# Attention by pairs of heads, with scores transposed, in a hybrid transformer layer

## The chip, the cores and the metric

The kernel runs on one core of a Trainium2 chip. The metric is the device time of one execution in microseconds (us): the median of the runs, each the time of that core. The core has five engines that run side by side, each with its own queue of instructions that it works off in order: TensorE (PE, matrix products, results in PSUM; PEld is its weight load), VectorE (DVE), ScalarE (ACT), GpSimd (POOL) and SyncE (SP), which here issues the transfers (DMAs) between the chip's memory and the core's SBUF.

## The reference

One layer over a prompt of 1024 tokens and a sample of 64 tokens that continues a cache of 256. A projection makes the columns of a recurrent mixer (RWKV, 8 heads of 64) and of a forgetting attention (FoX, 8 heads of 64); their outputs, side by side, go through one output projection, a gated residual, and a gated feed-forward part. The attention, which the change touches:

```python
s = einsum('bqhd,bshd->bhqs', q, k) * HEAD_DIM ** -0.5
decay_bias = lc_q[..., :, None] - lc_k[..., None, :]   # cumulated log-forget values
p = softmax(where(pos_k <= pos_q, s + decay_bias, -inf), axis=-1)
y_fox = einsum('bhqs,bshd->bqhd', p, v)
...
mix = concatenate([y_rwkv, y_fox], axis=-1) @ w_out
x = x + gt1 * mix
ffn = (silu(h2 @ w_ffn_gate) * (h2 @ w_ffn_up)) @ w_ffn_down
```

Everything is float32. The prompt attends to itself; the sample attends to the cache and to itself.

## The kernel before

The tokens are worked on in two halves: half 0 has prompt tokens 0 to 511, half 1 prompt tokens 512 to 1023 and the 64 of the sample (576 columns). The stages follow one another: conditioning and the projections of half 0 and half 1 (`pmm`, to 668.6 us of the profiled execution), attention of half 0, attention of half 1 with the output projection of half 0 among it (`po`, whose last matmul starts at 894.2), output projection of half 1, feed-forward (`pfa` to `pfe`), and `down`.

A projection multiplies in fp32r (a faster float format) with each operand split in a high and a low part: three matmuls a step, high by high, low by high, high by low (`mm3`, L322 to L324). Within the projections a written list, `ORDER`, sets in which order the parts of the recurrent mixer (A, B, D, N) and of q, k, v (Q, q, K, k, V) of each pair of heads are handed to the scheduler, which then interleaves their instructions on each engine. B3 is the chain of the last pair of the recurrent mixer (its matmuls are `pS` and `pY`), N3 its normalisation (`y`, `pbs`, `plora`), with which half 1's part of `yscr` is written. q and k go to memory as `qx` and `kx`, split in high and low (rows 0 to 63 and 64 to 127) with four rows for the forget bias; v goes to `vscr`, split too (`put_v`).

Attention goes head by head (`attend`, eight heads a half, units of 256 queries). For 128 queries: scores `psc` with queries on the partitions (two fp32r matmuls for each 512 or 256 keys, L957 and L959, and a mask, L963); the row's maximum by a DVE reduction (`nm`); exponential with the row sum on ACT (`p`); division by the sum (DVE or ACT); then 128x128 blocks of `p` are turned by fp32 transposes (`ppt`, L987), so that keys lie on the partitions, split in high (`pth`, ACT) and low (`ptl`, DVE), and multiplied with the split values (`pav`, L1009, two matmuls for each block of 128 keys; the weights hold 64 high and 64 low columns of v, so the two halves of the result are added at the end, `fy`). `Pipe(2)` lets three units overlap. Half 0's `fy` goes to `yscr` in memory (L1021), from where `load_mix` reads it back into `mixt`, two buffers in turn, and splits it into `mixrh`, `mixrl`, `mixfh`, `mixfl` for the output projection.

In half 1 every head has operands in two sets, which the transfers of the next head fill. After the units of each head stands one output tile of half 0's output projection (`outproj`: 8 tiles, 24 matmuls `po` each). `residual_x` reads the layer's input for the residual.

The SP queue issues all these transfers in order: a transfer that waits holds up those behind it.

## Time and profile before

| | |
|---|---|
| median of 3 runs | 1691.39 us (1688.1 to 1692.68) |
| the profiled execution | 1687.64 us; span of the instructions 1685.9 us |
| granted TensorE clock, mean | 0.991 |
| busy: PE / DVE / ACT / POOL | 1621.7 / 1107.1 / 731.5 / 130.4 us |
| bytes moved, mean rate | 207.05 MB, 123 GB/s |
| last projection matmul starts | 668.2 us |
| transfer of half 0's last `fy` issued | 734.4 us |
| last matmul of half 0's output projection starts | 894.2 us |

A row of the profile names the source line, engine, operation, result and operands, then the shape. Matmuls overlap, so that the duration of one is longer than its cost in a row of many: that cost is the distance from one start to the next.

### The profile page before, as it was taken

The page shows a single profiled execution, that of the slowest core. Times are in us where ns is not written, and L with a number is a line of the kernel's source. Part 1 is how long each engine was busy: PE and PEld are TensorE (multiplying, and loading weights), DVE is VectorE, ACT ScalarE, POOL GpSimd, SP SyncE. Part 2 cuts the span into 40 slices and gives each one's busy share as a digit, 9 for nine tenths or more (in the row PEclk, how much of TensorE's full clock was granted, in tenths as well). Part 3 has the DMA queues.
Part 4 walks back from the last instruction along what each step waited for, and adds up shares of the span by engine and source line. Part 5 has one row for each costly group of instructions (what it writes and reads, how often), then busy time and mean ns, then how long its engine had stood idle before and what let it go on. Part 6 is the DMA issues. An engine that isn't in the chain of part 4 may idle for free.

```text
span 1685.9 us, 32908 instructions
## 1 busy us (share of the span) xinstructions
PE 1621.7 (96%) x12959; PEld 1420.0 (84%) x12959; DVE 1107.1 (66%) x2397; ACT 731.5 (43%) x1496; POOL 130.4 (8%) x308
## 2 busy tenths in 40 slices
PE   5999999999999999879999999999999999999999
PEld 3666666688888888647889899999999999999998
DVE  6577676768876754868877975555555556545545
ACT  4543564653545445757766633233333333211210
POOL 0102101030211002002110000000000000000000
PEclk9999999999999999979999999999999999999999
DMA  7535366541233344576554532222222225423313
GB/s 309 161 101 156 108 180 206 173 124 44 60 86 96 94 117 116 178 212 167 153 162 164 187 104 77 78 77 78 77 78 78 77 65 188 140 84 97 97 41 122
DMA packets 133576, 207.05 MB, mean 123 GB/s; under 512 B 62126, under 2 KB 70350, under 8 KB 133422
## 3 DMA queue, kind: packets, MB, share of 16 engines
q1 hardware_dynamic: 133422, 204.95, 39.9%
q8 instruction: 102, 1.67, 0.4%
q14 instruction: 52, 0.43, 0.1%
HBM read 157.65 MB, written 47.25 MB: 122 GB/s over the span
## 4 chain that ended last, share of the span: by engine, by line
PE 58%; ACT 3%; DVE 2%; issue 1%; DMA 1%; SPq 0%; POOL 0%; DVEq 0%; ACTq 0%
PE pd L1322 15%; PE pfe L1207 8%; PE pfc L1207 8%; PE pfa L1207 8%; PE pfb L1207 4%; PE pav L1009 2%; PE ppt L987 2%; PE po L322 2%; PE po L323 2%; PE po L324 2%; PE psc L957 1%; PE psc L959 1%; ACT p L969 1%; PE pmm L322 1%; PE pmm L323 1%
## 5 line engine op out<-in xcount | busy, mean ns | idle before, releaser
L322 PE MATMUL pmm<-hhi,whi 128*128 128x288 f32 (+1 forms) x624 | 220.0, 353 | 6.0 <-ACT pb L345 4.6
L323 PE MATMUL pmm<-hlo,whi 128*128 128x288 f32 (+1 forms) x624 | 215.7, 346 | 1.8 <-DVE hlo L300 1.8
L324 PE MATMUL pmm<-hhi,wlo 128*128 128x288 f32 (+1 forms) x624 | 213.0, 342 | 0.2 <-DVE wlo L244 0.2
L240 ACT CAST whi<-wraw 128x1024 fp32r<-128x1024 f32 (+2 forms) x116 | 99.1, 855 | 205.8 <-PE pd L1322 164.0
L1322 PE MATMUL pd<-al,whi 128*128 128x512 f32 (+1 forms) x528 | 172.4, 327 | 0.0
L1322 PE MATMUL pd<-ah,whi 128*128 128x512 f32 (+1 forms) x528 | 172.2, 326 | 0.0
L1322 PE MATMUL pd<-ah,wlo 128*128 128x512 f32 (+1 forms) x528 | 172.2, 326 | 0.0
L1326 DVE SCALAR_TENSOR_TENSOR x1t<-pd,mod,x1t 128x512 f32<-128x512 f32 x192 | 91.1, 498 | 106.5 <-PE pd L1322 105.8
L322 PEld LDWEIGHTS pmm<-hhi,whi 128*128 128x128 f32 x624 | 118.5, 190 | 22.6 <-ACT pb L345 7.6
L323 PEld LDWEIGHTS pmm<-hlo,whi 128*128 128x128 f32 x624 | 118.5, 190 | 13.9 <-DVE hlo L300 2.8
L324 PEld LDWEIGHTS pmm<-hhi,wlo 128*128 128x128 f32 x624 | 118.3, 190 | 11.2 <-issue 1.7
L244 DVE TENSOR_TENSOR wlo<-wraw,whi 128x1024 fp32r<-128x1024 f32 (+2 forms) x108 | 104.0, 963 | 28.3 <-ACT whi L240 26.1
L1322 PEld LDWEIGHTS pd<-ah,whi 128*128 128x128 f32 x528 | 99.0, 188 | 7.1
L1322 PEld LDWEIGHTS pd<-ah,wlo 128*128 128x128 f32 x528 | 99.0, 188 | 7.1
L1322 PEld LDWEIGHTS pd<-al,whi 128*128 128x128 f32 x528 | 99.1, 188 | 7.0
L1207 PE MATMUL pfc<-hh,hS 128*128 128x256 f32 (+1 forms) x352 | 101.8, 289 | 1.1 <-ACT hh L1109 1.1
L1207 PE MATMUL pfa<-hh,whi 128*128 128x256 f32 (+1 forms) x352 | 102.0, 290 | 0.0
L1207 PE MATMUL pfc<-hh,lS 128*128 128x256 f32 (+1 forms) x352 | 101.8, 289 | 0.0
L1207 PE MATMUL pfa<-hl,whi 128*128 128x256 f32 (+1 forms) x352 | 101.7, 289 | 0.0
L1207 PE MATMUL pfa<-hh,wlo 128*128 128x256 f32 (+1 forms) x352 | 101.5, 289 | 0.0
L1207 PE MATMUL pfc<-hl,hS 128*128 128x256 f32 (+1 forms) x352 | 100.7, 286 | 0.0
L1154 ACT CAST hS<-wraw 128x512 fp32r<-128x512 f32 x88 | 53.6, 620 | 62.7 <-PE pfc L1207 61.5
(370 smaller groups left out, 4260.2 us busy)
## 6 DMA issues: line engine op xcount, KB each, us to landing
wraw<-in_w_in_dram SPq DMA_DIRECT2D x52, 512.0 KB
wada<-in_w_ada_dram SPq DMA_DIRECT2D x48, 512.0 KB
as<-actscr SPq DMA_DIRECT2D x22, 544.0 KB
wraw<-in_w_gate_dram SPq DMA_DIRECT2D x22, 512.0 KB
wraw<-in_w_up_dram SPq DMA_DIRECT2D x22, 512.0 KB
wraw<-in_w_down_dram SPq DMA_DIRECT2D x40, 256.0 KB
wraw<-in_w_out_dram SPq DMA_DIRECT2D x16, 512.0 KB
actscr<-sg SPq DMA_DIRECT2D x22, 288.0 KB
```

The costliest lines, as they stand in the source:

```text
L240: nc.scalar.copy(hi, src)
L244: eng.tensor_tensor(lo, src, hi.bitcast(F32), op=ALU.subtract)
L322: nc.tensor.matmul(ps[0:M, 0:n], whi[:, k, 0:M], xhi[:, k, off:off + n], start=(k == 0), stop=False)
L323: nc.tensor.matmul(ps[0:M, 0:n], whi[:, k, 0:M], xlo[:, k, off:off + n], start=False, stop=False)
L324: nc.tensor.matmul(ps[0:M, 0:n], wlo[:, k, 0:M], xhi[:, k, off:off + n], start=False, stop=(k == kt - 1))
L957: nc.tensor.matmul(pq[:, c:c + w], qs[:, q0 - t0:q0 - t0 + P], k1[:, k0 + c:k0 + c + w], start=True, stop=False, skip_group_check=True)
L987: nc.tensor.transpose(pt[0:rows, b - b0, t * P:t * P + qn], p[0:qn, pc:pc + rows], self.ident[0:qn, 0:qn])
L1009: nc.tensor.matmul(pv[:, 0:nq], w, pTs[b // 2][t][0:rows, b % 2, 0:nq], start=(b == 0 and t == 0), stop=(b == kb - 1 and t == 1))
L1154: nc.scalar.copy(w[x][0], src)
L1207: nc.tensor.matmul(ps, l[:, k], r[:, s, k], start=(first and k == 0 and y == 0), stop=(k == 3 and y == 2), skip_group_check=True)
L1322: nc.tensor.matmul(ps[:, 0:n], w[:, i], x[:, t:t + n], start=(i == 0 and y == 0), stop=(i == len(fs) - 1 and y == 2))
L1326: nc.vector.scalar_tensor_tensor(dst, ps[:, so - off:so - off + l], self.mod[:, 40 + o, b:b + 1], dst, op0=ALU.mult, op1=ALU.add)
```

## The change

Attention is worked off by pairs of heads. Scores are made twice. Once with the queries on the partitions in one fp32r matmul of 73 rows (`pmx`, high parts, the bias and a mask) only for the rows' maxima: DVE reduces each (`nmx`), one transpose (`pnm`) and two DVE operations put minus the maxima as further rows into the operand `qb`. Then transposed, keys on the partitions (`pst`, two fp32r matmuls and on the diagonal a mask), so that the exponential on ACT gives the weights as the value product needs them. The 312 transposes, the split of `p`, the split of v (`put_v`) and the division of each row go. The value product is plain fp32 on 64 columns a head, the two heads of a pair on column halves of the array (`pav`, 64x512); the weights are summed over the key blocks by adds one block behind (`acc`: in half 1 the second head's on POOL, else on DVE), a matmul with ones makes the sum over keys (`psm`), and one over it comes from ACT as exp(-ln). In half 1 `pss`, `pvs` are the sample's.

Half 0's pairs 0 to 2 stand in `ORDER` among half 1's last projections: `m` is the loads and maxima of a pair, `a` the rest. Pair 3 follows after them; half 1's pair 0 is loaded then, and its maxima stand beside pair 3. In half 1 (`att_second`) the order on PE is pinned as written: the maxima of the next pair and steps of three `po` matmuls stand among the blocks of the current pair, by the table `MIX`. There the operands `ka`, `qa`, `qb` of a head are single; `kb` and `qc` (for the maxima) are loaded one pair ahead. In the recurrent mixer the PSUM tag `ch` has one buffer instead of two; its place goes to `pv`.

```diff
         "Z0 T3 L D0 A0 ...
-... N1 V0 V1 B2 V2 Q2 N2 q2 K3 Q3 q3 P B3 K2 k3 k2 V3")
+... N1 V0 V1 B2 V2 Q2 N2 q2 m0 B3 K3 a0 Q3 q3 m1 K2 k3 a1 k2 V3 m2 N3 a2")
...
-            pm = [self.ps([P, 4, 2, 64], tag="ch", name="pM") for _ in range(2)]
+            pm = [self.ps([P, 4, 2, 64], tag=t, name="pM") for t in ("ch", "rb")]
...
-        self.put_v(j, vt, t0 // P, 4, P)
+        nc.sync.dma_start(self.vscr[j][:, t0 // P:t0 // P + 4], vt)
         if hf.smp:
-            self.put_v(j, vs.unsqueeze(1), 10, 1, SS)
+            nc.sync.dma_start(self.vscr[j][0:SS, 8], vs)
...
+    def att_get(self, j, hf):
...
+            g["tags"] = {"st": "st", "mx": "mx", "pv": "pv", "sm": "mx"}
...
+        k = self.rpool.tile([P, 4, 512], F32R, tag="At", name="ak")
+        g["ka"], g["kb"] = [k[:, h] for h in range(2)], [k[0:73, 2 + h] for h in range(2)]
+        t = self.rpool.tile([P, 4, 512], F32R, tag="kr", name="aq")
+        g["qa"], g["qb"] = [t[:, h] for h in range(2)], [t[0:73, 2 + h] for h in range(2)]
+        t = self.rpool.tile([P, 2, 512], F32R, tag="sv", name="qc")
+        g["qc"] = [t[0:73, h] for h in range(2)]
...
+        g["tags"] = {"st": "ra", "mx": "ra", "pv": "pv", "sm": "ra"}
+    def att_load(self, j, hf, g, part):
...
+            if part == 0:
+                ld(qc[0:64, 0:n], self.qx[hd, 64:128, q])
+                ld(qc[69:73, 0:n], self.qx[hd, 128:132, q])
+                ld(kb[0:64, 0:NK], self.kx[hd, 0:64, 0:NK])
+                ld(kb[69:73, 0:NK], self.kx[hd, 128:132, 0:NK])
+            elif part == 1:
+                ld(qb[0:64, 0:n], self.qx[hd, 0:64, q])
+                ld(qb[69:73, 0:n], self.qx[hd, 128:132, q])
+                for r in (0, 64):
+                    ld(qa[r:r + 64, 0:n], self.qx[hd, 64:128, q])
+                ld(ka[:, 0:NK], self.kx[hd, 0:128, 0:NK])
...
+    def att_max(self, j, hf, g):
+        nc, te = self.nc, self.te
+        nmx = self.nmx[j % 2]
+        kb, qc = g["kb"], g["qc"]
+        for h in range(2):
+            pc = self.tpool.tile([P, 4, 2], F32, tag="pc", name="pc") if hf.smp else None
+            for t in range(5 if hf.smp else 4):
+                smp = t == 4
+                qn, nk, k0 = (SS, 320, SP) if smp else (P, hf.t0 + (t + 1) * P, 0)
+                for x, c in enumerate(range(0, nk, 512)):
+                    m = min(512, nk - c)
+                    w = max(256, m)
+                    ps = self.ps([P, 512], tag=g["tags"]["mx"], name="pmx")
+                    te.matmul(ps[:, 0:w], qc[h][:, t * P:t * P + P], kb[h][:, k0 + c:k0 + c + w], start=True,
+                              stop=False, skip_group_check=True)
+                    if c + m == nk:
+                        d = 0 if smp else m - qn
+                        te.matmul(ps[0:qn, d:d + qn], self.identb[0:qn, 0:qn], self.cmask[0][0:qn, 0:qn], start=False,
+                                  stop=True, skip_group_check=True)
+                    dst = pc[:, t, x:x + 1] if hf.smp and not smp else nmx[0:qn, 32 * h + t:32 * h + t + 1]
+                    nc.vector.tensor_reduce(dst, ps[0:qn, 0:m], axis=AX.X, op=ALU.max, negate=True)
+                    yield
...
+    def att_rows(self, j, hf, g):
...
+        te.transpose(pt, self.nmx[j % 2], self.ident)
+        for h in range(2):
+            r = slice(32 * h, 32 * h + 5)
+            nc.vector.tensor_tensor(g["qb"][h][64:69, 0:nt * P].rearrange("p (t q) -> p t q", q=P),
+                                    pt[r].unsqueeze(1).to_broadcast([5, nt, P]),
+                                    self.ident[r, 32 * h:32 * h + nt].unsqueeze(2).to_broadcast([5, nt, P]), op=ALU.mult)
+    def att_main(self, j, hf, g):
...
+        blocks = [(b, max(0, b * P - t0)) for b in range(t0 // P + 4)]
+        acc = [g["acc"]() for _ in two]
+        pv = self.ps([P, 512], tag=tags["pv"], name="pav")
...
+        def scores(b, c0):
+            r = []
+            for h in two:
+                ps = self.ps([P, 512], tag=tags["st"], name="pst")
+                w = min(256, c0)
+                kc = slice(b * P, b * P + P)
+                diag = b * P >= t0
+                te.matmul(ps[:, w:512], ka[h][:, kc], qa[h][:, w:512], start=True, stop=False, skip_group_check=True)
+                te.matmul(ps[:, w:512], kb[h][:, kc], qb[h][:, w:512], start=False, stop=not diag, skip_group_check=True)
+                if diag:
+                    te.matmul(ps[:, c0:c0 + P], self.identb, self.cmask[1], start=False, stop=True, skip_group_check=True)
+                p = g["pt"]()
+                r.append((p, nc.scalar.activation(p[:, c0:512], ps[:, c0:512], AF.Exp)))
+                if h == 0:
+                    yield
+            done.append((b, c0, r))
+        def total(b, c0, r):
+            for h in two:
+                p, a = r[h][0], acc[h]
+                eng = nc.gpsimd if h and hf.smp else nc.vector
+                if b == 0:
+                    first.append(p)
+                elif b == 1:
+                    if c0:
+                        nc.gpsimd.tensor_copy(a[:, 0:c0], first[h][:, 0:c0])
+                    eng.tensor_tensor(a[:, c0:512], first[h][:, c0:512], p[:, c0:512], op=ALU.add)
+                else:
+                    eng.tensor_tensor(a[:, c0:512], a[:, c0:512], p[:, c0:512], op=ALU.add)
...
+        def values(group):
...
+                    mms.append(lambda b=b, c0=c0, h=h, p=p: te.matmul(
+                        pv[hs[h], c0:512], v[:, b, hs[h]], p[:, c0:512], start=(b == 0), stop=(b == blocks[-1][0]),
+                        skip_group_check=True))
...
+        done = []
+        for b, c0 in blocks:
+            for _ in scores(b, c0):
+                yield "h"
+            if len(done) > 1:
+                total(*done[-2])
+            yield "b"
+            if len(done) == 3:
+                values(done[:2])
+                del done[:2]
+            yield b
+        total(*done[-1])
+        values(done)
...
+        yield "v"
+        pd = self.ps([P, 512], tag=tags["sm"], name="psm")
+        for h in two:
+            te.matmul(pd[hs[h]], self.ones[:, 0:64], acc[h][:, 0:512], start=True, stop=True, skip_group_check=True)
+        fy = g["fy"]()
+        for c, m, a, d in ((0, 512, pv, pd),) + (((512, SS, pvs[:, 0], pvs[:, 1]),) if hf.smp else ()):
+            r = g["r"]()[:, 0:m]
+            nc.scalar.activation(r, d, AF.Ln)
+            nc.scalar.activation(r, r, AF.Exp, scale=-1.0)
+            nc.vector.tensor_tensor(fy[:, c:c + m], a, r, op=ALU.mult)
...
+    def proj_steps(self, hf):
...
+            for k in range(KT):
+                for y, (l, r) in enumerate(((wh, mh), (wh, ml), (wl, mh))):
+                    self.te.matmul(ps[:, 0:hf.n], l[:, k], r[:, k, 0:hf.n], start=(k == 0 and y == 0),
+                                   stop=(k == KT - 1 and y == 2))
+                if k == KT - 1:
+                    self.add_gated(ps, o, 16, hf, 0, hf.n)
+                yield
+    MIX = (1, 1, 1, 1, 1, 1, 1, 2)
+    def att_second(self, hf, h0):
+        fill = lambda it, n: [next(it, None) for _ in range(n)]
+        g = self.att_g
+        po = self.proj_steps(h0)
+        self.te.on = True
+        for j in range(4):
+            nxt, mx = None, iter(())
+            if j < 3:
+                nxt = self.att_get(j + 1, hf)
+                self.att_load(j + 1, hf, nxt, 0)
+                mx = self.att_max(j + 1, hf, nxt)
+            for b in self.att_main(j, hf, g):
+                if b == "v":
+                    if nxt:
+                        self.att_load(j + 1, hf, nxt, 2)
+                    fill(po, 4)
+                elif b in ("h", "b"):
+                    fill(mx, 1)
                 else:
+                    fill(po, self.MIX[b])
+                    fill(mx, b == 7)
+                if b == 7 and nxt:
+                    fill(mx, 99)
+                    self.att_load(j + 1, hf, nxt, 1)
+                    self.att_rows(j + 1, hf, nxt)
+                    fill(po, 2)
+            if j == 2:
+                self.load_mix(hf)
+            g = nxt
+        fill(po, 99)
+        self.te.on = False
...
+            self.att_ops(R(att, "attp", 1), 1)
+            self.tpool = MultiPool({t: R(att, "t" + t, b) for t, b in (("pc", 2),)})
+            self.att_pair(3, halves[0], "m")
+            self.att_g = g = self.att_get(0, halves[1])
+            for x in range(2):
+                self.att_load(0, halves[1], g, x)
+            main = self.att_main(3, halves[0], self.att0.pop(3))
+            mx = self.att_max(0, halves[1], g | {"tags": {"mx": "ra"}})
+            for b in main:
+                if b in range(4):
+                    for _ in range(5):
+                        next(mx, None)
             for b, f in late.values():
                 f(b())
+            self.att_rows(0, halves[1], g | {"tags": {"sm": "ra"}})
...
-            pb = {t: PB(att, "p" + t, b) for t, b in (("s1", 1), ("tr", 2), ("mm", 1), ("av", 1), ("s0", 1))}
+            self.pspool = MultiPool({t: PB(att, "p" + t, b) for t, b in (("st", 3), ("pv", 1), ("mm", 2), ("mx", 2))})
+            self.att_ops(R(att, "attp2", 1), 0)
+            self.att_load(0, halves[1], g, 2)
+            self.residual_x(halves[0])
+            self.load_mix(halves[0])
+            self.att_second(halves[1], halves[0])
```

Three places in the instructions' order. First PE about the last projection matmul. Before (`psc` is half 0's first head):

```order
2519 L322 MATMUL pmm<-hhi,whi 128x288
2520 L323 MATMUL pmm<-hlo,whi 128x288
2521 L661 MATMUL pS<-sv,kr 128x128
2522 L668 MATMUL pY<-kr,sv 128x128
2523 L324 MATMUL pmm<-hhi,wlo 128x288
2524 L861 MATMUL pkv<-ident,fv 128x128 x2
2525 L957 MATMUL psc<-k1x_7653,qsx_7651 128x256
2526 L959 MATMUL psc<-k2x_7654,q2x_7652 128x256
2527 L963 LDWEIGHTS identb
2528 L963 MATMUL psc<-cmask,identb 128x128
2529 L661 MATMUL pS<-sv,kr 128x128
2530 L668 MATMUL pY<-kr,sv 128x128
```

And now (`ak` and `qc` belong to half 0's pair 2; its maxima begin behind the last `pmm`, those of pairs 0 and 1 and their value products stand ahead of it):

```order
2660 L336 MATMUL pmm<-hhi,whi 128x288
2661 L337 MATMUL pmm<-hlo,whi 128x288
2662 L338 MATMUL pmm<-hhi,wlo 128x288
2663 L864 MATMUL pkv<-ident,fv 128x128 x2
2664 L1812 MATMUL pmx<-ak,qc 128x256
2665 L1812 LDWEIGHTS identb
2666 L1812 MATMUL pmx<-cmask_676,identb 128x128
2667 L1812 MATMUL pmx<-ak,qc 128x256
2668 L1812 LDWEIGHTS identb
2669 L1812 MATMUL pmx<-cmask_676,identb 128x128
2670 L417 MATMUL pbs<-y,bmean 128x288
2671 L1812 MATMUL pmx<-ak,qc 128x384
```

Where half 0's first head stood there is now its third pair.

Second, SP behind half 0's attention, from the transfers just before or at its last `yscr`. Before (`k1x`, `k2x`, `qsx`, `q2x`, `vsx` are half 1's first head's operands):

```order
412 L1043 DMA x_0_9112<-in_x_dram 128x1024 x3
413 L1031 DMA mixt<-yscr_71 128x512 x2
414 L915 DMA qsx_9133<-qx 128x576
415 L917 DMA k1x_9135<-kx 64x1344
416 L1021 DMA yscr_71<-fy 128x512
417 L917 DMA k1x_9135<-kx 64x1344
418 L920 DMA q2x_9134<-qx 64x576
419 L921 DMA k2x_9136<-kx 64x1344
420 L920 DMA q2x_9134<-qx 4x576
421 L921 DMA k2x_9136<-kx 4x1344
422 L923 DMA vsx_9137<-vscr_103 128x1280
423 L924 DMA vsx_9137<-vscr_103 64x128
```

And now (the operands of half 1's pair 0 have been issued ahead of these rows but for its values `vx`; `qcx_8489` and `kbx_8820` belong to pair 1):

```order
419 L1115 DMA yscr_71<-r_8723 128x512
420 L1200 DMA x_0_8772<-in_x_dram 128x1024
421 L1188 DMA mixt<-yscr_71 128x512
422 L958 DMA vx_8824<-vscr_103 128x1024
423 L959 DMA vx_8824<-in_cache_v_dram 128x256
424 L960 DMA vx_8824<-vscr_103 64x128
425 L1188 DMA mixt<-yscr_71 128x512 x2
426 L940 DMA qcx_8489<-qx 64x576
427 L940 DMA qcx_8489<-qx 4x576
428 L940 DMA kbx_8820<-kx 64x1344
429 L1188 DMA mixt<-yscr_71 128x512 x2
430 L940 DMA kbx_8820<-kx 4x1344
```

The read-back of half 0's output and its residual now stand ahead of the next pair's operands, where before a head's operands stood between them.

Third, PE at the start of half 1's attention. Before (behind the last `pav` of half 0):

```order
2794 L1009 MATMUL pav<-ptl,vsx_7660 128x256
2795 L322 MATMUL po<-mixrh_9116,whi 128x512
2796 L323 MATMUL po<-mixrl_9120,whi 128x512
2797 L324 MATMUL po<-mixrh_9116,wlo 128x512
2798 L322 MATMUL po<-mixrh_9116,whi 128x512
2799 L323 MATMUL po<-mixrl_9120,whi 128x512
2800 L324 MATMUL po<-mixrh_9116,wlo 128x512
2801 L957 MATMUL psc<-k1x_9135,qsx_9133 128x512 x2
```

And now (`pst` of pair 0, `pmx` of pair 1, then the first `po`):

```order
2835 L1812 MATMUL pss<-qbx_8496,kbx_8486 128x64
2836 L1812 LDWEIGHTS identb
2837 L1812 MATMUL pss<-cmask_683,identb 64x64
2838 L1812 MATMUL pst<-qax_8493,kax_8491 128x512
2839 L1812 MATMUL pst<-qbx_8495,kbx_8485 128x512
2840 L1812 MATMUL pmx<-kbx_8820,qcx_8489 128x512
2841 L1812 MATMUL pst<-qax_8494,kax_8492 128x512
2842 L1812 MATMUL pst<-qbx_8496,kbx_8486 128x512
2843 L1812 MATMUL pmx<-kbx_8820,qcx_8489 128x256
2844 L1812 LDWEIGHTS identb
2845 L1812 MATMUL pmx<-cmask_676,identb 128x128
2846 L1812 MATMUL po<-mixrh_8776,whi 128x512
```

The first `po` now stands behind two `pmx` of pair 1, which read `kbx_8820`.

370 lines of the change are left out of this document (163 added, 207 removed).

## The prediction

> **What bounds the kernel now.** I read the page's first part, then the table of stretches, then the edges of the stages in the timeline, then groups and waits.
>
> ```profile
> PE 1621.7 (96%) x12959; PEld 1420.0 (84%) x12959; DVE 1107.1 (66%) x2397; ACT 731.5 (43%) x1496; POOL 130.4 (8%) x308
> ```
>
> PE bounds the whole (96% of the span of 1685.9). By stage it does not (columns: stretch, length, busy PE, PEld, DVE, ACT, POOL, granted clock, DMA share, GB/s):
>
> ```profile
> 630.00:668.00 38.00, 37.73 (x469) 32.49 (x468) 12.28 (x22) 20.77 (x50) 8.90 (x11) 1.00 0.45 130
> 668.00:686.00 18.00, 15.75 (x88) 11.46 (x87) 15.35 (x49) 14.26 (x41) 3.52 (x8) 1.00 0.48 131
> 686.00:735.00 49.00, 38.86 (x225) 27.52 (x225) 39.26 (x120) 34.89 (x106) 5.29 (x31) 1.00 0.60 191
> 735.00:750.00 15.00, 9.04 (x25) 5.82 (x24) 4.21 (x8) 3.79 (x8) 0.00 (x0) 0.51 0.95 262
> 750.00:892.00 142.00, 140.80 (x845) 113.04 (x845) 110.76 (x230) 98.92 (x220) 24.56 (x39) 0.99 0.57 157
> ```
>
> The last projections (to 668) and half 1's attention with half 0's `po` (from 750) are full on PE. Half 0's attention (668 to 735) is a web of waits: PE and DVE each busy 54.6 of 67 us. Then comes a gap at half clock. Its edges:
>
> ```profile
> 668.60 0.36 PE L957 MATMUL psc<-k1x,qsx 128*128 128x256 f32 x1
> ...
> 734.42 0.53 SPq L1021 DMA_DIRECT2D yscr<-fy  x1
> ...
> 740.64 1.19 PE L957 MATMUL psc<-k1x,qsx 128*128 128x512 f32 x2 [3.86 <-DMA k1x<-kx]
> ...
> 750.17 0.63 PE L957 MATMUL psc<-k1x,qsx 128*128 128x512 f32 x1
> 750.60 0.63 PE L959 MATMUL psc<-k2x,q2x 68*128 68x512 f32 x1
> ...
> 894.20 0.39 PE L324 MATMUL po<-mixfh,wlo 128*128 128x512 f32 x1
> ```
>
> So half 0 takes 65.8 us (668.6, its first `psc`, to 734.4, its last output leaving); the restart waits for `k1x`, and its matmuls still start 0.43 apart at 750, twice the later distance; `po` of half 0 starts its last at 894.2 and is done by 894.4. Behind that nothing changes, so the forecast is how far 894.4 moves.
>
> **The change part by part.** Prices are distances between starts in undisturbed rows:
>
> ```profile
> 867.09 0.39 PE L957 MATMUL psc<-k1x,qsx 128*128 128x512 f32 x1
> 867.32 0.40 PE L959 MATMUL psc<-k2x,q2x 68*128 68x512 f32 x1
> 867.55 0.28 PE L957 MATMUL psc<-k1x,qsx 128*128 128x256 f32 x1
> 867.67 0.28 PE L959 MATMUL psc<-k2x,q2x 68*128 68x256 f32 x1
> 867.80 0.23 PE L963 MATMUL psc<-cmask,identb 128*128 128x128 bf16 x1
> 867.84 0.48 PE L957 MATMUL psc<-k1x,qsx 128*128 128x512 f32 x1
> ...
> 99.44 0.40 PE L324 MATMUL pmm<-hhi,wlo 128*128 128x512 f32 x1
> 99.77 1.06 PE L720 MATMUL pfl<-hhi,wfl 128*32 128x512 f32 x8
> 100.65 0.61 PE L720 MATMUL pfl<-hlo,wfl 128*32 128x512 f32 x4
> ```
>
> An fp32r matmul costs 0.23 for 512 columns, 0.12 for 256 (so about 0.18 for 384), a mask 0.04; 64-column ones I take as 0.11. `pfl` is plain fp32 on four column strips: eight records, that is four matmuls of 512 columns in two passes each, take 0.88 (99.77 to 100.65). So strips run side by side, and I price the two heads' `pav` at 0.85 for 512 columns together; bounds 0.85 and 1.7, if two strips behaved as one array. Entering strips cost 0.33 instead of 0.23 (99.44 to 99.77): 0.1 to 0.2 for each change of mode, taken 0.15. This change goes in and out 40 times in half 1, 6 us of the sum below.
>
> Half 0, one pair on PE: maxima 2 x (0.12+0.12+0.18+0.23) and 8 masks, 1.63; scores 2 heads x 2 terms x 0.65 and 8 masks, 2.93; values 1280 columns, 2.13; `psm` 0.85; `pnm` 0.2; six changes 0.9. Together 8.65. Pairs 0 and 1 lie whole ahead of the last `pmm`, in a stretch that is full: 17.3 us. B3's `pS` and `pY`, which before stood behind the last `pmm`, are now ahead: 4. For waits that the scheduler leaves there, 2 (0 to 6). So the start of what follows moves from 668.6 to 692.
>
> Behind it are pairs 2 and 3, N3 and the maxima of half 1's pair 0, chained through DVE and a PSUM ring of two (`ra`). DVE by these rows:
>
> ```profile
> L967 DVE TENSOR_REDUCE nm<-psc 128x1 f32<-128x512 f32 x8 | 5.4, 679 | 0.0
> L967 DVE TENSOR_REDUCE nm<-psc 128x1 f32<-128x384 f32 x8 | 4.4, 545 | 0.2 <-PE psc L963 0.2
> L967 DVE TENSOR_REDUCE nm<-psc 128x1 f32<-128x256 f32 x8 | 3.3, 414 | 0.0
> L967 DVE TENSOR_REDUCE nm<-psc 128x1 f32<-128x128 f32 x8 | 2.3, 285 | 2.1 <-PE psc L963 2.1
> L1001 DVE TENSOR_TENSOR ptl<-ppt,pth 128x512 fp32r<-128x512 f32 x8 | 5.5, 688 | 2.0 <-ACT pth L1000 2.0
> L969 ACT ACTIVATE p<-psc,nm 128x512 f32<-128x512 f32 x8 | 5.5, 690 | 0.1
> ```
>
> Maxima of two pairs 4 x 1.92 = 7.7; of half 1's pair 0, 2 x (4 x 0.679 + 1.92 + about 0.48 for the sample) = 10.2; N3's six operations about 3.5; twelve adds of 384, 256 and 128 columns about 5; two `fy` and six rows of maxima at 0.69 about 5.5. That is 32 us on DVE, the lower bound. The upper is 52: 34 reductions each waiting some 0.35 us more for a ring of two, and 8 of serial steps. For each pair maxima, `pnm`, `qb`, scores, exponentials, `psm`, ln, exp and `fy` follow one another; two such tails of about 6 us beside the 32 make 44, nearer the lower end since DVE has other work in most of them. The last `fy` comes at 692 + 44 = 736, against 734.4.
>
> Then SP. In its order stand `yscr`, residual, `mixt`, `vx`, two `mixt`, `qcx`, `kbx` (64 rows), two `mixt`, `kbx` (4 rows): 3.3 MB. The third and fifth `mixt` wait for the split of the first and third (two buffers). PE, pinned, does `pss` and one `pst` and then needs `kbx`.
>
> ```profile
> 739.13 1.76 SPq L1031 DMA_DIRECT2D mixt<-yscr  x2
> ...
> 747.55 0.32 SPq L1031 DMA_DIRECT2D mixt<-yscr  x1
> ...
> 734.00:752.00 18.00, 11.59 (x31) 7.50 (x32) 6.01 (x10) 5.19 (x10) 0.39 (x4) 0.53 0.86 236
> ```
>
> At 236 GB/s 3.3 MB take 14.0 us; before, the third `mixt` came 8.4 us behind the first. I take 14 (6 if the transfers find free engines and SP is not held, 17 if two splits cost 8.4 each): first `pmx` at 750. PE will idle some 12 us, and as before (740.64 to past 750) run its next 9 us at half clock: 4.5 lost.
>
> From there PE's work is, in half 1 with `po`: 192 `po` 44.7; `pst` 4 x 6.6 (20 of 512, 4 of 384, 8 of 256, 8 masks); `pmx` of three pairs 12.8; `pav` 3328 columns a pair, 4 x 5.5; `pss` 42 x 0.11 = 4.8; `psm` 3.4; `pvs`, `pnm` 2.2; mode changes 6. Sum about 122.5, of which 2 are done before the stall. Before, the 874 attention and `po` matmuls of that stage, priced alike, sum to 133.5; from about 752, at full clock, they took 142 for the 128 then left: 1.11 of the prices. Fewer hand-overs between engines here (no transposes to split) let me take 1.05 (1.0 to 1.11): 126.5.
>
> ```profile
> L244 POOL TENSOR_TENSOR mixfl<-fy,mixfh 128x576 fp32r<-128x576 f32 x4 | 6.4, 1606 | 15.2 <-ACT mixfh L240 15.2
> ```
>
> No other engine is the bound there: for each pair (about 31 us) DVE has 10.2 of maxima, 4 of adds, some 3.5 of residual and `fy`; POOL seven adds, at 1.6 for 576 columns 1.4 or less each, and the splits; ACT sixteen exponentials of 0.69 or less and the splits. Between pairs `ka`, `qa`, `qb` are single: they load only when the last `pst` is done, 2.3 MB, 9.7 us at 236 GB/s, while PE has eight `po` steps (5.6) and the last values and sums (2.4): 1.7 short, three times, 5 in all (0 to 8).
>
> Without cost: `put_v`'s DVE work leaves a stretch where DVE is busy 12.28 of 38; `ch` with one buffer delays a chain that `pmm` covers (0 to 5 if that cover fails). Half 1's last split is covered by the six `po` steps left behind it.
>
> Sum: 736, +14 = 750, +4.5 for the clock, +126.5 less 2.1 done before, +5 between pairs: 884, 10.4 earlier than 894.4. The profiled execution took 1687.64 (1.7 outside its span), so 1677.2; it stands 3.75 below the median of 1691.39, so 1681.
>
> **Rivals.**
> 1. The transition is shorter: the reductions keep DVE full (32 us), and the transfers stall PE 6. The end moves by a further 12 + 8: 1661. For it: the DMA engines were free for half of 668 to 735 (share 0.48 to 0.60). Against: `mixt` waits for splits by its two buffers.
> 2. Slower: the pinned order on PE. Each block hands PE two `pmx` that wait for a DVE reduction, queued behind an add that itself waits for an exponential. At 0.8 us a block over 32 blocks that is 26 us: 1707. It decides from 0.47 us a block (15 us) on. For it: before, `psc` waited for ACT in half 0 (below). Against: three `st` and two `mx` buffers.
>
> ```profile
> PE psc L957 <- ACT p L969: 5.0, 12, 1.2
> ```
>
> 3. The two heads do not run side by side: 22 us in half 1 and about 6 before it, 1709. `pfl` speaks against.
> 4. No change: each change of mode empties the array, for the 0.39 us that one matmul lasts at 99.44. 40 changes in half 1 and 12 among the projections then cost 0.24 more each, 12.5: 1693.5. Against: 99.44 to 99.77 is 0.33 with the matmul itself. By the Trainium skill, TensorEngine Tiling (Array Packing), Key Properties, changing the tiling mode drains TensorE; the row agrees that a change costs, but with 0.1 beyond the matmul.
>
> **How the numbers follow.** My forecast's own range is 1674 to 1689, chance 0.42; rival 1, 0.20; rival 2, 0.20 (1691 to 1707, a quarter of it within 0.3%); rival 3, 0.06; rival 4, 0.12. About 0.3% (5 us) is what a measurement here can tell from no change. Faster: 0.20 and 0.86 of 0.42, 0.56; same: the rest of 0.42, rival 4 and a quarter of rival 2, 0.22; slower: 0.22. The range 1658 to 1703 leaves out some of rivals 1 and 2 and rival 3.
>
> **What the profile would show.** Right: last `pmm` near 692, last `yscr` near 736, a PE gap of about 12 us behind it ended by `kbx`, pairs of `pav` records 0.01 apart, three short gaps ended by `ka`, `qa` or `qb`, `po`'s last start near 884. Wrong: `pav` of 512 columns 0.85 apart for each head; many waits of `pmx` for DVE or `pst` for ACT behind 750; a last `yscr` ahead of 728 or behind 746.

## The result and the profile after

The changed kernel took 1730.19 us (median of 4 runs, 1727.16 to 1735.05) against 1690.95 (4 runs of the kernel before beside it): 1.0236 times as long, 95% interval 1.0209 to 1.0264. I had forecast 1681, from 1658 to 1703. The profiled execution took 1735.05, the longest of the four; its span is 1732.9, 47.0 longer than before.

The first part of the page:

```profile
PE 1642.2 (95%) x12783; PEld 1402.2 (81%) x12783; DVE 1061.4 (61%) x2174; ACT 664.2 (38%) x1284; POOL 171.7 (10%) x304
```

DVE and ACT lost 46 and 67 us of work as meant, PE's busy time grew by 20.5. The edges of the stages, from the timelines of PE and SP:

```profile
713.66 0.29 PE L338 MATMUL pmm<-hhi,wlo 128*128 128x288 f32 x1
...
776.22 0.33 SPq L1115 DMA_DIRECT2D yscr<-r  x1
...
791.17 0.77 PE L1812 MATMUL pmx<-kbx,qcx 73*128 73x512 f32 x1 [12.28 <-DVE mixrl L258]
...
938.80 0.39 PE L1812 MATMUL po<-mixfh,wlo 128*128 128x512 f32 x1
939.03 0.29 PE L336 MATMUL po<-mixrh,whi 128*128 128x288 f32 x1
```

Half 0's last `po` ends its turn at 939.0. Against the forecast (`lq_undone` is an experiment, explained below):

| stage | before | forecast | after | `lq_undone` |
|---|---|---|---|---|
| last projection, then what follows | 668.6 | 692 | 713.9 | 695.3 |
| from there to the last `yscr` | 65.8 | 44 | 62.3 | 62.1 |
| from there to the first `pmx` of half 1's pair 1 | | 14 | 15.0 | 15.6 |
| from there to the end of half 0's `po` | | 134 | 147.8 | 147.9 |
| sum of the last three | 225.8 | 192 | 225.1 | 225.6 |

What stands behind half 0's `po` is 2.4 longer than before. So the loss is 45.3 us up to the last projection, where I expected 23.4, and none of the 34 that I expected to win behind it came. The table of stretches for that part, before (668.6 to 894.6) and after (713.9 to 939.2), the transition ahead of the first `po`, the rest, and both together:

```profile
668.60:734.50 65.90, 53.51 (x307) 37.95 (x304) 53.95 (x165) 48.47 (x147) 8.55 (x37) 1.00 0.57 177
734.50:894.60 160.10, 152.94 (x882) 121.44 (x883) 115.37 (x237) 103.61 (x229) 25.98 (x40) 0.95 0.60 164
668.60:894.60 226.00, 206.45 (x1188) 159.39 (x1186) 169.31 (x402) 152.08 (x375) 34.54 (x77) 0.96 0.59 168
```
```profile
713.90:792.90 79.00, 53.60 (x191) 29.54 (x189) 36.83 (x70) 18.09 (x35) 10.05 (x13) 0.65 0.56 159
792.90:939.20 146.30, 137.75 (x686) 88.88 (x686) 79.92 (x122) 53.12 (x101) 50.90 (x38) 0.94 0.45 132
713.90:939.20 225.30, 191.35 (x874) 118.42 (x873) 116.74 (x192) 71.21 (x136) 60.95 (x51) 0.84 0.49 141
```

Busy PE times granted clock, as a rough measure of the work at full clock, is 206.45 x 0.96 = 198 before and 191.35 x 0.84 = 161 after. So 37 us of work left this part, about what I had forecast (34); by the forecast's prices some 21 of it only moved ahead of the last projection (pairs 0 and 1, and B3). In its place came waits and work at a lower clock: the clock is 0.65 over the 79 us of the transition, where it was 1.00.

Ahead of that, the time was lost in one place in half 0's projections. The 313th of the `pmm` matmuls started at 166.3 before and at 192.2 after. Of these 26 us 20 to 26 stayed most of the time (15 for a while), and 23.1 at the 1717th, which starts at 644.4. The stretches from 170 to 190 of before, then of after:

```profile
170.00:180.00 10.00, 9.43 (x77) 5.73 (x77) 8.54 (x16) 8.27 (x16) 0.71 (x1) 1.00 0.38 96
180.00:190.00 10.00, 10.00 (x170) 7.56 (x169) 8.49 (x17) 5.59 (x14) 1.71 (x2) 1.00 0.60 191
```
```profile
170.00:180.00 10.00, 4.07 (x16) 2.23 (x14) 8.91 (x15) 7.88 (x15) 0.72 (x1) 0.74 0.35 88
180.00:190.00 10.00, 5.45 (x36) 2.88 (x34) 5.59 (x10) 1.71 (x5) 0.00 (x0) 0.50 0.37 115
```

PE runs out of weights. SP's queue shows why; of the rows from 138 to 179 us, before then after, those that bring weights (`wraw`), wait long, or write the constants (`cones`):

```profile
143.28 0.58 SPq L310 DMA_DIRECT2D wraw<-in_w_in_dram  x1
152.11 0.38 SPq L310 DMA_DIRECT2D wraw<-in_w_in_dram  x1
156.01 0.54 SPq L310 DMA_DIRECT2D wraw<-in_w_in_dram  x1
166.36 0.43 SPq L310 DMA_DIRECT2D wraw<-in_w_in_dram  x1
178.14 0.33 SPq L310 DMA_DIRECT2D wraw<-in_w_in_dram  x1
179.74 0.33 SPq L693 DMA_DIRECT2D yscr<-y  x1
```
```profile
138.36 0.58 SPq L324 DMA_DIRECT2D wraw<-in_w_in_dram  x1
138.98 1.47 SPq L717 DMA_DIRECT2D qx<-cones  x4
155.84 0.31 SPq L553 DMA_DIRECT2D dw<-wb  x1
157.78 0.66 SPq L717 DMA_DIRECT2D kx<-cones  x2
172.86 0.34 SPq L707 DMA_DIRECT2D yscr<-y  x1
...
178.93 0.39 SPq L324 DMA_DIRECT2D wraw<-in_w_in_dram  x1
```

Before, five loads of weights are issued between 143 and 179, all ahead of `yscr`. After, none is from 138.36 to 178.93: SP stands at `dw` and at `yscr`, and the next load is behind both. The waits of SP there:

```profile
SPq L553 <- DVE wb L546: 15.3, 1, 15.3
SPq L707 <- DVE y L705: 14.4, 1, 14.4
```

The line behind it is one that the prediction passed over, since it is neither attention nor a queue (it is in the diff, but not among the lines of it shown above): the log-forget table `lq` moved from a tile of its own into the general ring of slots, which has one buffer here. `ones_rows` (O in `ORDER`) takes the tile `cones`, from which constants are written to `qx` and `kx`, from the same ring. In the two traces these writes moved from 56.5 to 111.8 us to 139.0 to 173.2 us, and the load of weights to behind the waiting `yscr`.

### The profile page after: what moved, and what is told of

It is laid out like the page before. It is cut to its first block, busy times and chain, and to the rows that moved or that the text cites. A ratio compares the mean times of both kernels' runs of the same rounds, so it can differ in the third digit from the quotient of the medians.

```text
span 1732.9 us, 31993 instructions
## 1 busy us (share of the span) xinstructions
PE 1642.2 (95%) x12783; PEld 1402.2 (81%) x12783; DVE 1061.4 (61%) x2174; ACT 664.2 (38%) x1284; POOL 171.7 (10%) x304
## 4 chain that ended last, share of the span: by engine, by line
PE 77%; DVE 8%; ACT 4%; DMA 4%; issue 1%; SPq 0%; DVEq 0%; ACTq 0%
PE pd L1479 15%; PE pfe L1364 7%; PE pfc L1364 7%; PE pfa L1364 7%; PE pmm L336 4%; PE pfb L1364 4%; PE pmm L337 4%; PE pmm L338 4%; PE po L1812 3%; PE pst L1812 3%; PE pav L1812 2%; PE pbs L417 2%; PE pmx L1812 2%; PE pS L675 1%; PE po L338 1%
## 5 line engine op out<-in xcount | busy, mean ns | idle before, releaser
L1026 ACT ACTIVATE pT<-pst 128x512 f32<-128x512 f32 (+3 forms) x96 | 46.1, 490 | 84.8 <-PE pst L1812 77.9
```

The lines of the kernel that those rows point to most:

```text
L1026: r.append((p, nc.scalar.activation(p[:, c0:512], ps[:, c0:512], AF.Exp)))
```

## The experiments

All are timed beside the kernel before on the same chip; ratios are to that, with 95% intervals. First the four runs on the ring `lq` shares and on the buffer of `ch`.

**The table's ring alone, in the kernel before** (`lq_alone`).

```diff
-        q4 = self.fpool.tile([P, 7, 4, 8], F32, tag="lq", name="lq")
+        q4 = self.slot([P, 7, 4, 8], name="lq")
```

> The kernel before, with one line of the change alone: the log-forget table lq is taken from the one-buffer ring that the rows of ones (cones) also use. Theory A (that line turns SP's order round in the first half's projections: cones wait for lq, and yscr then stands ahead of the next projection weights): the 24 us loss near 166 to 192 us appears here too, time 1710 to 1720. Theory B (the loss comes from the one ch buffer in the recurrent mixer): no change, 1691 within 4.

Measured: 1728.59 against 1690.15, ratio 1.0233 (1.0202 to 1.0265): 38 us from one line, more than theory A had allowed. It is as much as the changed kernel lost, but not the same loss: there only 10 us come back when the line's effect on the order is undone (next run). In the trace of `lq_alone` SP issues no load of `wraw` between 125.19 and 179.66. The 313th `pmm` is 24.7 late, the last one 39.3; of the rest most is added to the matmuls that stood from 510 to 546 before, where this kernel's clock is 0.63 and then 0.51 (550 to 570 in its trace, against 1.00). What brought the clock down there is not shown.

**The same line in the changed kernel, its effect on the order undone** (`lq_undone`): the constants are handed over ahead of the log-forget step. This is the base of most runs below.

```diff
-ORDER = ("Z0 D0 A0 D1 Z1 L Q0 B0 V0 N0 A1 C0 Z2 D2 q0 O A2 ...
+ORDER = ("Z0 D0 A0 D1 Z1 O L Q0 B0 V0 N0 A1 C0 Z2 D2 q0 A2 ...
```

> The changed kernel with one token moved in the first half's ORDER: the rows of ones (O) are handed over ahead of the log-forget part (L), so that cones no longer wait for lq. Theory A: the 24 us go, 1703 to 1709. Theory B: 1730, as the changed kernel.

Measured: 1720.07, ratio 1.0181 (1.0146 to 1.0216), 10 us less than the changed kernel by the medians. By the two profiled executions it is 18.4, all of it ahead of the last projection (713.9 to 695.3), but these are the longest of four runs and the shortest of four. In its trace four loads of `wraw` are issued again between 142 and 177 us, and the 1717th `pmm` starts at 619.9 (621.3 before, 644.4 after). So the hole is closed. I had expected 1703 to 1709, because I took the loss behind the projections for smaller.

**The constants first, in the kernel before with the table's ring** (`lq_alone_rows_first`): both edits above, without the rest of the change.

> The kernel before with the log-forget table in the ring of slots (1728.6 alone), and the rows of ones (O), which write constants out from that same one-buffer ring, ahead of the log-forget step (L) in the first half's order. Theory A (the 38 us come from the order on SP's queue: the constants wait for the ring, and the weights' loads stand behind them): with the constants ahead the loads stand as before, and the time is 1690 to 1696. Theory B (the table costs in the ring itself, in both halves, whatever stands behind it: 24.7 us of the 39.3 lay in the first half's projections, the rest in the second's, where no constants are written): 1700 to 1712.

Measured: 1696.47, ratio 1.0044 (1.0024 to 1.0065). Of 38 us 31 are gone, so it is the order on SP's queue, theory A: three loads of `wraw` are issued between 143 and 162 us again, and the clock is 1.00 from 510 to 560. 7 to 8 us stay, just beyond what I allowed. No run gives `lq` its own tile back in the changed kernel, so what stays there is not measured.

**One buffer for `ch` alone, in the kernel before** (`ch_alone`).

```diff
-            pm = [self.ps([P, 4, 2, 64], tag="ch", name="pM") for _ in range(2)]
+            pm = [self.ps([P, 4, 2, 64], tag=t, name="pM") for t in ("ch", "rb")]
...
-                                     "ch": E(psA, "psch", 2, space=PSUM)})
+                                     "ch": E(psA, "psch", 1, space=PSUM), "pv": E(psA, "pspv", 1, space=PSUM)})
...
```

> The kernel before, with the PSUM tag ch at one buffer alone (pM on ch and rb, the freed bank named pv and used in the conditioning). Theory A: within 6 us of 1691. Theory B: 1710 to 1720.

Measured: 1699.13, ratio 1.0047 (1.0025 to 1.0069), 8 to 9 us, a little more than theory A allowed and far from theory B. The last projection ends only 1.1 later. The last `pS` of B3, which in that kernel runs behind the projections, ends at 685.9 and not at 673.6, and what follows is 4.3 late at the first `po` and 9.7 at the last.

**Two buffers for `ch` in the changed kernel** (`ch_undone`; here `lq` stands as in the changed kernel).

```diff
...
-                                     "ch": E(psA, "psch", 1, space=PSUM), "pv": E(psA, "pspv", 1, space=PSUM)})
-            self.pspool.alias = {"ps": "ra"}
+                                     "ch": E(psA, "psch", 2, space=PSUM)})
+            self.pspool.alias = {"ps": "ra", "pv": "fx"}
...
```

> The changed kernel with the ring ch at two buffers again; the sums of a pair (pv) share the ring fx instead, and the log-forget table stands where the change put it (1730.2 without this edit). I had costed one buffer at nothing (0 to 5 us). Theory A (in the changed order the state's chain of the last block lies among projections, so one buffer costs nothing, though it cost 8.2 us put alone into the kernel before, where that chain ran behind the last projection): within 3 us, 1727 to 1733. Theory B (the 8 us are paid here too): 1720 to 1724.

Measured: 1728.68, ratio 1.0237 (1.0212 to 1.0263), the same as the changed kernel. By the times one buffer costs nothing that can be told where B3 stands among projections, and 8 to 9 us where it did not: theory A. The profiled execution is not quite so clean: with two buffers B3's last `pS` ends at 697.5 and not at 709.5, and the stage from the last projection to the last `yscr` takes 56.0 us and not 62.3. Part of B3's delay may thus reach that stage; times 1.5 us apart can't settle it.

Now the stretch behind the last projection, all on the base of `lq_undone` (1.0181).

**Another ring for the maxima** (`max_ring_mm`). Half 1's first maxima and half 0's last pairs share the two buffers of `ra`; the ring `mm` of the projections is idle then.

```diff
-            mx = self.att_max(0, halves[1], g | {"tags": {"mx": "ra"}})
+            mx = self.att_max(0, halves[1], g | {"tags": {"mx": "mm"}})
```

> The changed kernel with the order of the log-forget table undone (1720.1), and beside that the maxima of the second half's first pair take the ring of PSUM tiles that the projections have left idle (mm) and not the ring ra, which the scores and maxima of the last two pairs of the first half use too. Theory A (the stretch from the last projection to the last write of the row scratch, 62 us against my 44, is a chain of PE, VectorE and two shared buffers): the stretch shortens by 8 to 14 us, to 48 to 54, and the time falls to 1706 to 1712. Theory B (the stretch is long because TensorE runs at half its clock there, 0.56 to 0.58 granted, whatever the rings): 0 to -3 us, 1717 to 1721, and the clock in the stretch stays where it was.

Measured: 1708.35, ratio 1.0101 (1.0070 to 1.0133), 12 us less. The last projection ends at 693.7, and from its timelines:

```profile
737.87 0.35 SPq L1115 DMA_DIRECT2D yscr<-r  x1
...
761.44 0.77 PE L1812 MATMUL pmx<-kbx,qcx 73*128 73x512 f32 x1 [5.71 <-DMA kbx<-kx]
...
763.17 0.78 PE L1812 MATMUL po<-mixrh,whi 128*128 128x512 f32 x1
```

The last `yscr` comes 44.2 behind the last projection and not 62, though the clock stays low (0.83, 0.70, 0.50 from 700 to 760). So the shared ring held that write. But the 44.2 are not the 44 of my forecast, for which half 1's first maxima stood ahead of the write; here they end behind it. The work as a whole is done when these maxima are turned (`pnm`), in `lq_undone`, then here:

```profile
754.53 0.42 PE L1815 MATMUL pnm<-ident,nmx 128*64 128x128 f32 x1
```
```profile
750.19 0.42 PE L1815 MATMUL pnm<-ident,nmx 128*64 128x128 f32 x1 [0.65 <-DMA mixt<-yscr]
```

That is 59.2 behind the last projection in `lq_undone` and 56.5 here: 3 us for the work, where the write won 18. Of the 10 us that are left at the first `po` the other 7 come, by these traces, from the loads, which follow the write and now run under the maxima: from half 1's first `pst` to the first `po` it takes 8.7 us where `lq_undone` took 15.8. The loads of pair 1 are still waited for.

**Extra matmuls that keep TensorE busy** (`warm`).

```diff
+                    if hf.smp and j == 0:
+                        wps = self.ps([P, 512], tag="mm", name="pwarm")
+                        for _ in range(3):
+                            te.matmul(wps[:, 0:512], qc[h][:, 0:P], kb[h][:, 0:512], start=True, stop=True,
+                                      skip_group_check=True)
```

> The same base (1720.1), with three extra matmuls of 73x128 by 73x512 behind each maximum's matmul of the second half's first pair; their results are not used. 54 matmuls at 0.23 us are 12.6 us of added work at the full clock and 23 us at half. Theory B (the clock fell because TensorE has gaps there): with the gaps filled the granted clock from 725 to 760 us rises from 0.57 to 0.8 or more, and the stretch gets shorter by 2 to 8 us in spite of the added work: 1712 to 1718. Theory A (a chain over two buffers): the clock may rise, the stretch stays or grows by 0 to 5 us. If the clock stays at half, it grows by 10 to 20 us: 1730 to 1740.

Measured: 1722.67, ratio 1.0194 (1.0144 to 1.0245). The stretch from 740 to 760 of `lq_undone`, then of this kernel:

```profile
740.00:760.00 20.00, 17.28 (x60) 10.17 (x59) 10.88 (x23) 3.04 (x7) 1.65 (x2) 0.58 0.32 104
```
```profile
740.00:760.00 20.00, 20.00 (x91) 12.66 (x89) 9.43 (x19) 2.28 (x6) 0.00 (x0) 0.85 0.25 71
```

The clock rose from 0.58 to 0.85, as theory B says (from 720 to 740 it stayed at 0.55); the stretch to the last `yscr` went from 62.1 to 68.7, as theory A allows or a little more, and the whole did not get faster. PE is now busy for all 20 us, so the added work itself fills this stretch: the run does not tell what the low clock cost before.

**The same with the ring free** (`four_edits_warm`, on the kernel `four_edits` below, 60 extra matmuls).

```diff
+    def warm(self, a, b, n):
+        ps = self.ps([P, 512], tag="fx", name="pwarm")
+        for _ in range(n):
+            self.te.matmul(ps, a, b, start=True, stop=True, skip_group_check=True)
...
+                    if hf.smp and j == 0:
+                        self.warm(qc[h][:, 0:P], kb[h][:, 0:512], 2)
...
+                if not hf.smp and j == 3:
+                    self.warm(ka[h][:, kc], qa[h], 3)
```

> The four edits (1703.8), with 60 extra matmuls of 128x512 whose results are not used, two behind each maximum of the second half's first pair and three behind each pair of score matmuls of the first half's last pair. They are 14 us of TensorE time at the full clock, 26 at half. Theory A (with the shared ring gone the stretch of 44 us is bound by TensorE at half its clock, busy for 15.9 and 16.8 of 20 us at 0.79 and 0.67 granted): with the gaps filled the clock rises to 0.9 or more from 700 to 760, the stretch from the last projection to the first projection step of the next part shrinks by 3 to 8 us, 1696 to 1701. Theory B (a chain of score, exponential or reduction, and loads sets it): the clock rises and the time grows by 2 to 8 us, 1706 to 1712. If the clock does not rise, it grows by 12 to 20.

Measured: 1707.97, ratio 1.0104 (1.0081 to 1.0127), against 1.0075 for the four edits. The transition of `four_edits`, then of this kernel:

```profile
690.50:764.30 73.80, 61.90 (x219) 35.26 (x217) 38.04 (x74) 19.22 (x38) 13.08 (x15) 0.70 0.56 158
```
```profile
693.10:772.20 79.10, 73.47 (x278) 43.80 (x277) 38.70 (x74) 19.19 (x38) 13.11 (x15) 0.78 0.50 148
```

The clock rises only from 0.70 to 0.78 (0.94 from 740 to 760, but 0.74 from 700 to 740), and the stage is 5.3 longer, though the profiled execution of `four_edits` is the shortest of its six. In neither run did filling the gaps pay. What the stage would take at full clock without the added work, these runs don't tell.

**The keys of pair 1 first** (`keys_first`).

```diff
-                nxt = self.att_get(j + 1, hf)
-                self.att_load(j + 1, hf, nxt, 0)
+                nxt = self.att_n if j == 0 else self.att_get(j + 1, hf)
+                if j:
+                    self.att_load(j + 1, hf, nxt, 0)
...
+            self.att_n = self.att_get(1, halves[1])
+            self.att_load(1, halves[1], self.att_n, 0)
             self.residual_x(halves[0])
             self.load_mix(halves[0])
```

> lq_undone, and pair 1's kbx and qcx are handed over ahead of the residual and of the read-back of half 0's output. If PE's 12 us stall behind half 0's last yscr is SP's order (my reading of the trace), the first pmx of pair 1 starts some 7 us behind yscr instead of 15, and the time falls by 6 to 10 against lq_undone. Rival: PE then waits for the split of mixt at its first po instead, and the time falls by 0 to 2.

Measured: 1721.57, ratio 1.0192 (1.0158 to 1.0227): nothing won, as the rival said. Its timeline:

```profile
769.83 0.77 PE L1815 MATMUL pmx<-kbx,qcx 73*128 73x512 f32 x1 [7.88 <-DMA kbx<-kx]
...
775.46 0.79 PE L1815 MATMUL po<-mixrh,whi 128*128 128x512 f32 x1 [3.67 <-ACT mixrh L254]
```

The stall ahead of pair 1 shrank from 13.5 (start to start, in `lq_undone`) to 8.5, and a new wait of 4 us came at the first `po`, whose rows now load behind the keys. PE's order is pinned, so the later of the two counts.

**Keys first, rows ahead of the residual, `po` from the fourth block on** (`keys_and_steps_later`).

```diff
-    MIX = (1, 1, 1, 1, 1, 1, 1, 2)
+    MIX = ((0, 0, 0, 1, 2, 2, 2, 2), (1, 1, 1, 1, 1, 1, 1, 2))
...
-            self.residual_x(halves[0])
             self.load_mix(halves[0])
+            self.residual_x(halves[0])
```

> Keys of the second half's second pair handed over first, as in the run before (1721.6: the first matmul of that pair came 5 us sooner after the last write, then the first projection step waited 4.0 us for its rows), and now the rows of the first half's result loaded ahead of the residual, and no projection steps in the first three blocks of that pair; they stand in the later blocks. Theory A (the stall of 13.5 us has two chains behind it, the keys and the projection's rows, and taking only one of them away moved the wait): both waits shrink, the first step waits under 1 us, and 5 to 8 us are won against the base: 1712 to 1715. Theory B (transfers bound the stretch, whatever their order: share of the DMA engines 0.73 to 0.9 there): the wait turns up in a third place and the time is 1718 to 1722.

Measured: 1715.01, ratio 1.0145 (1.0112 to 1.0178). The first `pmx` of pair 1 starts 8.1 behind the last `yscr` and the first `po` waits for nothing:

```profile
766.03 0.77 PE L1815 MATMUL pmx<-kbx,qcx 73*128 73x512 f32 x1 [5.44 <-DMA kbx<-kx]
...
778.39 0.48 PE L1815 MATMUL po<-mixrh,whi 128*128 128x512 f32 x1
```

In the profiled executions half 0's `po` ends 4.2 sooner than in `lq_undone`. Theory A by the trace; the times say 5 us, with intervals that overlap.

**The steps at the borders of the pairs spread** (`boundaries`).

```diff
-                    fill(po, 4)
+                    fill(po, 2)
...
-                    self.att_rows(j + 1, hf, nxt)
                     fill(po, 2)
+                    self.att_rows(j + 1, hf, nxt)
+            fill(po, 2)
```

> The same base (1720.1); at the border of two pairs in the second half, two projection steps stand ahead of the transpose of the maxima (pnm) and two ahead of the next pair's sample scores (pss) instead of all ahead of the sums. Theory A (the three waits of 2.3, 3.0 and 1.2 us at pnm and of 1.3 us three times at pss are stalls of an order that gives TensorE nothing to do there, and my 5 us between pairs were too few): the waits fall by 5 to 9 us in all, 1711 to 1715. Theory B (the pairs are bound by VectorE, ScalarE or the transfers between, and PE only waits elsewhere): within 2 us, 1718 to 1722.

Measured: 1715.97, ratio 1.0145 (1.0112 to 1.0179), 4 us by the medians, within the uncertainty. PE's waits from the first `po` to its end, in the changed kernel (793 to 939), then here (778 to 926):

```profile
PE pnm L1815 <- DVE nmx L988: 5.9, 3, 2.8
PE pss L1812 <- ACT r L1109: 1.4, 2, 0.7
PE pss L1812 <- DMA vx<-vscr: 0.7, 1, 0.7
PE pmx L1812 <- DVE pc L985: 0.5, 1, 0.5
```
```profile
PE pmx L1813 <- DMA kbx<-kx: 5.2, 2, 2.8
PE pnm L1816 <- DVE nmx L988: 1.8, 2, 1.2
PE pss L1813 <- DMA kax<-kx: 1.1, 1, 1.1
```

8.5 us of waits became 8.1: what waited for the maxima now waits for the next pair's loads. From the first `po` to the end of half 0's `po` it took 147.7, against 146.2 in `lq_undone`. In the time theory A is not excluded, in the trace B holds.

**Four edits together** (`four_edits`: constants first, maxima on `mm`, keys first with the later steps, borders), **and the third pair earlier** (`four_edits_pair2_early`).

```diff
-         "... m0 B3 K3 a0 Q3 q3 m1 K2 k3 a1 k2 V3 m2 N3 a2")
+         "... m0 B3 K3 a0 Q3 q3 m1 K2 a1 k3 m2 k2 a2 V3 N3")
```

> Four edits of the runs before together, on the changed kernel: the order of the log-forget table undone (1720.1 alone), the maxima of the stretch on the idle ring (11.7 us less), keys first and projection steps later (5.1 less), the steps at the borders of the pairs spread (4.1 less, within its uncertainty). Theory A (the places are apart, and each gain stands by itself): 1720.1 - 11.7 - 5.1 - 4.1 = 1699.2, range 1696 to 1703. Theory B (what the ring frees comes back behind the last write, where the loads of keys, values, residual and rows share the DMA queues, 25 us from that write to the first projection step in the ring's run; and the waits at the borders pass to the loads of the next pair, 672 KB per head): the later edits add under 4 us, 1704 to 1709.

> The four edits, and the third pair of the first half (m2 and a2) stands before the last values' projection (V3 N3) and not behind it, so that its scores and sums run between dense projections. Theory A (the stretch behind the last projection is long by the pair's work at half the clock, 0.57 to 0.83 granted): the last projection ends 6 to 10 us later, the first projection step of the next part comes 4 to 8 us sooner than that shift, and the time is 3 to 8 us under the four edits. Theory B (the pair's work is hidden in neither place, and only changes sides): within 3 us of the four edits.

Measured: 1703.80, ratio 1.0075 (1.0050 to 1.0101), between the two theories; and 1698.64, ratio 1.0065 (1.0042 to 1.0089), not to be told from it. In the second the last projection ends 6.1 later and the transition is 7.0 shorter: the pair's work changed sides. Neither beats the kernel before; by the ratios they take back about two thirds of the loss.

## Why the prediction was wrong

The forecast's end of half 0's `po` was 884, measured 939.0. Three terms failed: `lq` was left out, and the transition and the steady part were sized too small. The 55 us by step, in the profiled executions, of which that of the changed kernel stands 4.9 above its median and that of `lq_undone` 3.8 below:

- **A line that was not costed: 18.6 us at the last projection (10 by the medians).** The part on `ch` and `put_v` treats what the change does to buffers in the projections, but `lq`, in the same diff, stands nowhere. It costs no instruction; it changed which transfer stands ahead of which. That is shown: alone 38 us, with the constants first 7 to 8.
- **The pairs among the projections: right, 3.3 more.** 668.6 to 692 was forecast; with the queue mended it is 695.3, and 697.8 at most in the other runs with this order.
- **`ch` at no cost: right by the times**, for the reason given, that B3 is covered, though the trace of `ch_undone` leaves it open whether the cover is complete. Where it is not covered it cost 8 to 9, more than the 5 of my upper bound.
- **The transition, 44 us: wrong by 18.3.** VectorE's work was sized right (32; it was busy for 31.0). The forecast then added 12 us of tails and no more, "since DVE has other work in most of them" (it calls its 44 nearer the lower end; it lies above the middle of 32 to 52). VectorE had no such work: it stood idle for half of the stage. TensorE stands nowhere in that sum, and its clock is charged only behind the stall. It was busy for 49.2 of 62.3 us at a clock of 0.69 (the row below this list). The product, 34 us, is my estimate of the same work at full clock, so up to 15 of the 18 us could be the clock. The ring of two, which the text had in its upper bound, held the last write for 18 us, but the work for only 3. How the 18 divide between clock, waits and ring no run separates, and why the clock fell here stays open.
- **14 us to the first `pmx`: right** (15.0), wait and length; the 12.28 of idle time is the 12 that I named. The profile puts it down to a split (`mixrl`), but handing over the keys first shortened it by 5 us. It was two chains, and the forecast had written both down without saying that removing one shows the other.
- **The steady part, 134 us: wrong by 14.** Busy PE times clock is 137.75 x 0.94 = 129.5 from 792.9, against 124.4; PE idles 8.5 where I had 5; and 137.75 - 129.5 = 8.3 is low clock, where I had 4.5 for the whole stage. The clock fell again at the first two borders of pairs (0.73 from 820 to 826, 0.72 from 860 to 866, 0.63 from 872 to 880), not at the third; I charged it once. In 1.7 us more, the first `pmx` and `pst` pass ahead of the first `po`. The 124.4 also holds a slip: 122.5 less the 2 done before, times 1.05, is already the 126.5, and the sum takes 2.1 off again. By its own terms it comes to 886.

The changed kernel's transition, from the last projection to the last `yscr`:

```profile
713.90:776.20 62.30, 49.18 (x177) 26.45 (x175) 31.04 (x62) 13.92 (x28) 8.75 (x12) 0.69 0.51 143
```

The price of packing was right. Eight `pav` of the two heads, then a step of `po`, in the changed kernel's timeline:

```profile
837.88 0.23 PE L1812 MATMUL pmx<-cmask,identb 128*128 128x128 bf16 x1
838.04 1.94 PE L1812 MATMUL pav<-pT,vx 128*64 128x512 f32 x8
839.91 0.50 PE L1812 MATMUL po<-mixrh,whi 128*128 128x512 f32 x1
840.25 0.39 PE L1812 MATMUL po<-mixrl,whi 128*128 128x512 f32 x1
840.48 0.39 PE L1812 MATMUL po<-mixrh,wlo 128*128 128x512 f32 x1
```

The eight records are two key blocks of both heads, two passes for each matmul. From the first to the `po` behind them 1.87 us pass: two blocks at the 0.85 that I had priced, 1.70, and 0.17 more; one head after the other they would take 3.4, so **rival 3** is out. Going into strips takes 0.16 behind the mask instead of 0.04, and the `po` behind them 0.34 instead of 0.23. With the 0.17 that is 0.40 for in and out, 0.2 for each change where I took 0.15. **Rival 4** (0.39 each) is out. **Rival 2** in its own place, waits of `pmx` for DVE in each block of half 1, is out with 0.5 us in all; its mechanism, reductions on too few buffers, shows in the transition instead, where `pmx` waits 3.3 us in all for maxima. **Rival 1** needed a transition shorter than 44. None of the four is what came.

On the clock the trace shows how a stall goes on costing. Behind the 12.28 us of idle time ahead of 791.17, matmuls of 512 columns start 0.43 apart (794.33, 794.75, 795.18, 795.61). From 795.61 on, 4.4 us behind the first, the distance shrinks, and at 797.20 it is 0.23:

```profile
795.18 0.63 PE L1812 MATMUL pmx<-kbx,qcx 73*128 73x512 f32 x1
795.61 0.57 PE L1812 MATMUL pst<-qax,kax 128*128 128x512 f32 x1
...
797.20 0.39 PE L1812 MATMUL pst<-qax,kax 128*128 128x512 f32 x1
797.43 0.40 PE L1812 MATMUL pst<-qbx,kbx 73*128 73x512 f32 x1
```

The Trainium skill, TensorE: Matmul & The Clock Gate, Part 1, says that the full clock returns after one busy window of about 3.4 us, and that the window runs freely. The trace agrees: the 4.4 us fit one such window and part of the one in which the matmuls began.

## What to carry to other kernels

Read every line of a diff for the ring it allocates from, above all where a ring has one buffer: a tile that moves costs no instruction and can reorder a queue, and here the next projection's weights then stood behind transfers that waited 15 and 14 us. When work goes off a bound engine, price the stage that is left by its waits and by the clock that the engine is granted there, not by the work: here 37 us of TensorE work left the part, and it kept its length. A write that comes sooner is not a stage that ends sooner: on another ring the write won 18 us and the work 3. And where two inputs are waited for in an order that is pinned, price both, since speeding up one only moves the wait to the other.

## What was not expected of the hardware

The granted clock stayed between 0.56 and 0.83 from 700 to 780 us in `lq_undone`, in stretches of 20, though PE counted as busy for 53 of the 79 us from the last projection to the first `po`, and though up to 759 no wait was longer than 3.3 us. In the kernel before, PE was busy for 53.5 of 65.9 us in the same place, and the clock was 1.00. These runs don't show why. Raising it with extra matmuls to 0.85 and 0.94 in single stretches of 20 us made neither kernel faster. And one buffer of PSUM less cost nothing that the times show in one order of the work, and 8 to 9 us in another.
